# Gates by logarithm, exponential and a Newton step, and linear-attention steps at quarters of a chunk, in a two-layer hybrid encoder on one core

## The chip, the cores and the metric

The kernel runs on one core of one Trainium2 chip. The metric is the device time of one execution in microseconds (us). The engines are called by the profile's names: PE (TensorE matmuls), PEld (TensorE weight loads), ACT (ScalarE), DVE (VectorE), POOL (GpSimd) and SP (SyncE, which issues the DMAs here).

## The reference

Two encoder layers work on 272 tokens (256 and 16 learned meta tokens), model width 2048, all in float32. In each layer one projection makes the inputs of two groups of heads; their outputs are concatenated, projected, added to the residual and normalised; a squared-ReLU MLP of width 8192 and a second LayerNorm follow.

```python
def _layer(h, w_in, ...):
    proj = jnp.einsum('bld,dp->blp', h, w_in)
    gq, gk, gv, gr, glr, nq, nk, nv = jnp.split(proj, points, axis=-1)
    y_gla = _gla_mixer(gq, gk, gv, gr, glr, gla_w_up, gla_b_up, gla_norm_w)
    y_na = _na_mixer(nq, nk, nv, na_rel_bias)
    mix = jnp.einsum('blm,md->bld', jnp.concatenate([y_gla, y_na], axis=-1), w_out)
    h = _layer_norm(DEEPNORM_ALPHA * h + mix, ln1_w, ln1_b)
    ff = jnp.einsum('blf,fd->bld', jnp.square(jax.nn.relu(jnp.einsum('bld,df->blf', h, w_ff1))), w_ff2)
    return _layer_norm(DEEPNORM_ALPHA * h + ff, ln2_w, ln2_b)

# _gla_mixer, four heads, both directions: S_t = diag(a_t) S_{t-1} + k_t^T v_t,  o_t = q_t S_t
    o = (o_fwd + o_bwd)[:, pad:].reshape(B, L, GLA_HEADS, GLA_DV)
    o = o * lax.rsqrt(jnp.mean(jnp.square(o), axis=-1, keepdims=True) + LN_EPS) * norm_w
    o = o.reshape(B, L, GLA_HEADS * GLA_DV) * jax.nn.silu(r)
```

The neighbourhood attention (NA, 16 heads) lets each of the 4 x 64 grid tokens attend to a clamped window and to the meta tokens, with a relative bias. The meta tokens are dropped at the end, so layer 1 (the second) needs 256 columns of most results.

## The kernel before, in words

Activations lie as (128 features, tokens). A large product is made in three matmuls of rounded operands: high weight by high and by low activation, low weight by high activation (`three`, L151 to L162). With 272 columns these are L160, L161 and L162; with 256 columns high and low activations lie side by side and L156 takes both, L157 the third. A product of 128 output rows runs over 16 chunks of 128 input features, called chunks here.

**The weight stream.** Weights arrive as tiles of 128 x 1024 floats, eight chunks each. `made` (L137) issues a tile's DMA on SP, ACT casts its high part (`wh`, L147), DVE subtracts for the low part (`wl`, L148). `raw`, `wh` and `wl` have three buffers each, and `weights` keeps one tile ahead of the one in use.

**Background work.** `by_m` (L190) runs the products of one group of 512 output rows. After each eighth chunk and after each eviction it calls `pump(fg, bg)`, which adds to two credits and takes one step of the queue `fg` or `bg` per whole credit; a step is one stretch of a generator up to its `yield`. A step's instructions are placed in each engine's program behind the stream's so far, and DVE's behind the newest `wl` (`issue_after`). A builder with priorities settles the final order of each engine's instructions and the waits.

**The stage around the change.** After keys, values and queries, each layer runs two groups of 512 columns for the output gate r (`ev_r`), with `pump=(1, GLA_R)`, then six groups for NA (`ev_na`), with `pump=(1, GLA_NA)`. Beside them `bg` holds the whole linear attention (`gla`, L479), and `fg` the gates (`silu`, L417) and then the NA pairs (`na_pair`, L590). Before the sixth NA group whatever is left in `bg` is taken at once.

`gla` computes the scores of each of four heads by ten levels, distance classes in powers of two. A level is a chain over four engines: POOL makes differences of the running decay (`gaps`, L460; L447 to L450 at level 9), ACT takes their exponential (L471), DVE multiplies by q and k (L476), PE makes the scores (L505, and L507 for the meta rows; L498 and L500 at level 9), and DVE or ACT puts them into A by a mask (L519, L521). The chain runs ahead: two `gaps` and one `operands` are issued before their level's matmuls; the tile `lev` has three buffers. Scores with the 16 meta keys are collected in `Am`. At the end of a head `gla_out` (L529) zeroes a tile `am` on POOL (L533), stacks `Am` in it as high, low and high part (`stack`: ACT L214 twice, DVE L215), and in the next steps multiplies by the values (L542, L543 with A, L544 with `am`), takes the mean square (L776), and applies the norm, the gate and the rounding.

**The gate.** `ev_r` takes exp(-r) from PSUM on ACT (L411, tile `rs`), POOL adds one (L412), ACT copies r (L414, tile `rv`); `silu` inverts in two halves on DVE (L421) and multiplies by r (L424). There are eight gates a layer, 16 in all. `newton` (L427) is the LayerNorm's and `gla_out`'s inverse root: logarithm and exponential on ACT (L429, L430), and three DVE operations (L431 to L433). The one table set that ACT loads at the start holds both functions.

Of the kernel before, what the change touches and what calls it, by code (L numbers as in the profile page):

```python
# [2 lines left out]

# [11 lines left out]
P = 128  # L15
# [16 lines left out]
EPS = 1e-5  # L32
TAU = 16.0
NEG = -1e30
GLA_R, GLA_NA, NORMS = 1.3, 1.1, (1.0, 0.6)
LEAD = 4


# [9 lines left out]
class Trunk:  # L48
# [18 lines left out]
    def consts(self):  # L67
        nc, c = self.nc, self.cp
        t = lambda n, s, d=F32: c.tile(s, d, name=n, tag=n)
        self.vec = t("vec", [P, DEPTH, 66])  # L70
        nc.sync.dma_start(self.vec, self.i["vec"].rearrange("l p v -> p l v"))
        self.ident = t("ident", [P, P])
        nc.sync.dma_start(self.ident, self.i["ident"])
        self.sel = t("sel", [LRK, 2])
        nc.sync.dma_start(self.sel, self.i["sel"])
        self.qmask = t("qmask", [NM, NK2])
        nc.sync.dma_start(self.qmask, self.i["qmask"])
        self.mask = t("mask", [P, 7, P], U8)
        raw = self.wp.tile([P, WB], F32, name="raw", tag="raw")[:, :7 * P].rearrange("p (l c) -> p l c", l=7)
        nc.sync.dma_start(raw, self.i["mask"])  # L80
        nc.gpsimd.tensor_copy(self.mask, raw)
        self.ones = {}
        for n in (GDV, 4 * P, D):
            self.ones[n] = t(f"ones{n}", [P, P])
            nc.gpsimd.memset(self.ones[n], 1.0 / n)
        self.ones_r = {}
        for n in self.ones:
            self.ones_r[n] = t(f"onesr{n}", [P, P], F32R)
            nc.scalar.copy(self.ones_r[n], self.ones[n])
        self.eps = t("eps", [P, 1])  # L90
        nc.gpsimd.memset(self.eps, EPS)
        self.one = t("one", [P, 1])
        nc.gpsimd.memset(self.one, 1.0)

# [95 lines left out]
    def by_m(self, acts, ns, evict, pump=(0, 0), apart=False, renew=False):  # L190

        nk = len(acts)
        for m, n in enumerate(ns):
            ps = self.pm.tile([P, 512], F32, name="mm", tag="mm")
            for k in range(nk):
                if k % 8 == 0:
                    wh, wl = self.weights()
                self.three(ps, wh, wl, (k % 8) * P, acts[k], n, k == 0, k == nk - 1)
                if k % 8 == 7 and k < nk - 1:
                    self.pump(*pump)  # L200
                if renew and m == len(ns) - 1 and k == 8:
                    self.renew(2)
            parts = [ps[:, :T], ps[:, T:]] if n == T else [ps[:, :n]]
            evict(m, parts if apart else self.whole(parts))
            self.pump(*pump)

    def split(self, src, hi, lo):
        self.nc.scalar.copy(hi, src)
# [197 lines left out]
    def ev_r(self, c, ps):  # L406

        nc, n = self.nc, self.n
        self.y[c] = self.pair(self.yp, "y", c)
        s = self.g2.tile([P, L], F32, name="rs", tag="rs")[:, :n]  # L410
        nc.scalar.activation(s, ps, AF.Exp, scale=-1.0)  # L411
        nc.gpsimd.tensor_scalar(s, s, 1.0, 1.0, ALU.mult, ALU.add)  # L412
        r = self.g2.tile([P, L], F32, name="rv", tag="rv")[:, :n]
        nc.scalar.copy(r, ps)  # L414
        self.fg.append(self.silu(c, s, r))

    def silu(self, c, s, r):  # L417
        yield
        half = self.n // 2
        for p in (slice(0, half), slice(half, self.n)):  # L420
            self.nc.vector.reciprocal(s[:, p], s[:, p])  # L421
            yield
        gate = self.g2.tile([P, L], F32, name=f"gate{c}", tag=f"gate{c}", bufs=1)[:, :self.n]
        self.nc.vector.tensor_tensor(gate, r, s, ALU.mult)  # L424
        self.gate[c] = gate

    def newton(self, y, v, eps, t):  # L427
        nc = self.nc
# [50 lines left out]
    def gla(self):  # L479

        nc, n, full, g2 = self.nc, self.n, self.full, self.g2
        levels = (7, 0, 1, 2, 3, 4, 5, 6, 8, 9)
        todo = iter([(h, lv) for h in range(GH) for lv in levels])
        begun = [self.gaps(*next(todo)) for _ in range(2)]
        yield
        ahead = self.operands(*begun.pop(0))
        yield  # L490
        for h in range(GH):
            A = g2.tile([P, 6, P], F32, name="A", tag="A")
            Am = g2.tile([NM, L], F32, name="Am", tag="Am")
            for lv in levels:
                q, k = ahead
                ps = self.bank()
                if lv == 9:
                    nc.tensor.matmul(ps[:, :T], lhsT=k[:, T:T + P], rhs=q[:, :T], start=True, stop=True)  # L498
                    for b in range(2 * full):
                        nc.tensor.matmul(ps[:, T + b * NM:T + b * NM + NM], lhsT=k[:, b * P:b * P + P],  # L500
                                         rhs=q[:, T:L], start=True, stop=True)
                else:
                    for b in (slice(0, P), slice(P, T)):
                        r = b if lv < 8 else slice(P - b.start, T - b.start)
                        nc.tensor.matmul(ps[:, b], lhsT=k[:, b], rhs=q[:, r], start=True, stop=True)  # L505
                    if full and lv <= 4:
                        nc.tensor.matmul(ps[:, T:L], lhsT=k[:, T:T + P], rhs=q[:, T:L], start=True, stop=True)  # L507
                if begun:
                    ahead = self.operands(*begun.pop(0))
                nxt = next(todo, None)  # L510
                if nxt:
                    begun.append(self.gaps(*nxt))
                p2 = ps[:, :T].rearrange("p (s c) -> p s c", s=2)
                if lv == 9:
                    if full:
                        nc.vector.tensor_copy(A[:, 2:6:3, :NM], ps[:, T:T + 2 * NM].rearrange("p (s c) -> p s c", s=2))
                    nc.scalar.copy(Am[:, :T], ps[:NM, :T])
                elif lv >= 7:
                    nc.scalar.copy(A[:, 0:5:4, :] if lv == 7 else A[:, 1:4:2, :], p2)  # L519
                else:  # L520
                    nc.vector.copy_predicated(A[:, 0:5:4, :], self.mask[:, lv:lv + 1, :].to_broadcast([P, 2, P]), p2)  # L521
                if full and lv == 0:
                    nc.vector.tensor_copy(Am[:, T:L], ps[:NM, T:L])
                elif full and lv <= 4:
                    nc.vector.copy_predicated(Am[:, T:L], self.mask[:NM, lv, :NM], ps[:NM, T:L])
                yield
            yield from self.gla_out(h, A, Am)

    def gla_out(self, h, A, Am):  # L529

        nc, n, g2 = self.nc, self.n, self.g2
        am = g2.tile([80, L], F32R, name="am", tag="am")[:, :n]
        nc.gpsimd.memset(am.bitcast(F32), 0.0)  # L533
        self.stack(Am[:, :n], am, NM, (0, 64), 32)
        yield
        af = A.rearrange("p s c -> p (s c)")
        os_ = []
        sq = g2.tile([P, 2, L], F32, name="sq", tag="sq", bufs=1)
        for e in range(2):
            o = self.bank()[:, :n]  # L540
            c = slice(h * GDV + e * P, h * GDV + e * P + P)
            nc.tensor.matmul(o, lhsT=self.V[0][:, c], rhs=af[:, :n], start=True, stop=False)  # L542
            nc.tensor.matmul(o, lhsT=self.V[1][:, c], rhs=af[:, 384:384 + n], start=False, stop=False)  # L543
            nc.tensor.matmul(o, lhsT=self.VS[:, c], rhs=am, start=False, stop=True)  # L544
            nc.scalar.activation(sq[:, e, :n], o, AF.Square)
            os_.append(o)
            yield
        nc.vector.tensor_tensor(sq[:, 0, :n], sq[:, 0, :n], sq[:, 1, :n], ALU.add)
        ms = yield from self.mean(sq[:, 0, :n], GDV, pool=g2)
        rs = g2.tile([P, L], F32, name="grs", tag="grs", bufs=1)[:, :n]  # L550
        tn = g2.tile([P, L], F32, name="gtn", tag="gtn", bufs=1)[:, :n]
        self.newton(rs, ms, self.eps, tn)
        yield
        while 2 * h + 1 not in self.gate:
            yield
        for e in range(2):
            c = 2 * h + e
            hi, lo = (t[:, :n] for t in self.y[c])
            o = g2.tile([P, L], F32, name="on", tag="on")[:, :n]
            nc.vector.scalar_tensor_tensor(o, os_[e], self.vec[:, self.l, 64 + e:65 + e], rs, ALU.mult, ALU.mult)  # L560
            nc.vector.tensor_tensor(o, o, self.gate[c], ALU.mult)
            self.split(o, hi, lo)
            self.done.add(c)
            yield
# [458 lines left out]
```

## Time and profile before

| what | value |
|---|---|
| median of 3 runs | 2427.96 us (2427.77 to 2428.14) |
| the profiled execution | 2427.82 us, of which the span is 2425.8 us |
| granted clock, mean | 0.997 |
| layer 0: gate stage, NA and linear attention, to the output projection | about 110 to 380 us |
| layer 1: the same | about 1352 to 1600 us |
| HBM read | 412.57 MB, 171 GB/s with the writes over the span |

In a row of the profile's groups stand line, engine, operation, output and inputs, shapes and count, then busy us and mean ns of one, then the idle time of the engine just before them and what ended it. In a timeline row the start and duration in us come first, and a bracket gives the idle time before and what ended it. A list of waits gives who waited for whom, us in total, times and the longest. Idle time of an engine that is not the bottleneck costs nothing; the chain of work that ended last lies on PE for 94% of the span.

### The profile page before, as it was taken

What the parts mean: (1) busy time and instruction counts of PE and PEld (TensorE: products, weight loads), DVE (VectorE), ACT (ScalarE), POOL (GpSimd) and SP (SyncE); (2) the same over time, 40 slices, a digit from 0 to 9 for tenths busy, and PEclk for the clock granted to TensorE, in tenths of its full rate; (3) what the DMA queues carried; (4) which work ended last, traced back from release to release, by engine and by line L of the source; (5) the groups of instructions that cost most, each with busy time, mean ns of one, the idle gap of its engine ahead of it and who ended that gap; (6) DMA issues with size and microseconds to landing.
All of it is one profiled execution on the core that took longest, in us unless ns stands there. A gap on an engine that the chain in (4) does not pass through costs nothing.

```text
span 2425.8 us, 43082 instructions
## 1 busy us (share of the span) xinstructions
PE 2394.4 (99%) x17276; PEld 2270.6 (94%) x17276; DVE 1576.3 (65%) x2469; ACT 1189.2 (49%) x1962; POOL 285.7 (12%) x447
## 2 busy tenths in 40 slices
PE   9999999999999999999999999999999999999997
PEld 9999999999999999999999899999988888888886
DVE  6688777775544455546577787778866555666655
ACT  6555555564433344444456555555644333444443
POOL 1064420010000000000021444300200000000000
PEclk9999999999999999999999999999999999999998
DMA  7544444555555555555555444456566556556563
GB/s 243 165 133 155 145 133 158 172 179 175 174 175 174 175 177 174 177 175 173 176 168 186 144 156 150 136 156 191 184 190 184 190 189 187 189 185 189 186 189 129
DMA packets 118359, 417.46 MB, mean 172 GB/s; under 512 B 13388, under 2 KB 16332, under 8 KB 118160
## 3 DMA queue, kind: packets, MB, share of 16 engines
q1 hardware_dynamic: 118160, 414.72, 54.1%
q8 instruction: 135, 2.21, 0.4%
q14 instruction: 64, 0.52, 0.1%
HBM read 412.57 MB, written 2.10 MB: 171 GB/s over the span
## 4 chain that ended last, share of the span: by engine, by line
PE 94%; DVE 3%; issue 1%; ACT 1%; DMA 0%; POOL 0%; SPq 0%; ACTq 0%; DVEq 0%; POOLq 0%
PE mm L156 22%; PE mm L160 17%; PE mm L162 17%; PE mm L161 17%; PE mm L157 11%; PE mm L186 5%; PE bg L505 1%; DVE wl L148 1%; PE bg L652 1%; DVE acc L868 1%; PE bg L601 0%; POOL lev L460 0%; ACT wh L147 0%; PE bg L322 0%; PE bg L542 0%
## 5 line engine op out<-in xcount | busy, mean ns | idle before, releaser
L148 DVE TENSOR_TENSOR wl<-raw,wh 128x1024 fp32r<-128x1024 f32 (+1 forms) x772 | 946.0, 1226 | 654.6 <-ACT wh L147 646.2
L147 ACT CAST wh<-raw 128x1024 fp32r<-128x1024 f32 (+1 forms) x772 | 805.1, 1044 | 956.6 <-PE mm L161 405.6
L160 PE MATMUL mm<-x,wh 128*128 128x272 f32 (+2 forms) x2176 | 632.6, 291 | 0.0
L161 PE MATMUL mm<-x,wh 128*128 128x272 f32 (+2 forms) x2176 | 628.4, 289 | 0.0
L162 PE MATMUL mm<-x,wl 128*128 128x272 f32 (+2 forms) x2176 | 628.4, 289 | 0.0
L160 PEld LDWEIGHTS mm<-x,wh 128*128 128x128 f32 x2176 | 413.3, 190 | 1.4 <-issue 0.5
L162 PEld LDWEIGHTS mm<-x,wl 128*128 128x128 f32 x2176 | 410.6, 189 | 0.3
L161 PEld LDWEIGHTS mm<-x,wh 128*128 128x128 f32 x2176 | 410.0, 188 | 0.1
L156 PE MATMUL mm<-x,wh 128*128 128x512 f32 x1152 | 408.7, 397 | 0.0
L157 PE MATMUL mm<-x,wl 128*128 128x256 f32 x1152 | 324.5, 282 | 0.3 <-DVE wl L148 0.3
L156 PEld LDWEIGHTS mm<-x,wh 128*128 128x128 f32 x1152 | 217.7, 189 | 49.8 <-issue 0.6
L156 PE MATMUL mm<-y,wh 128*128 128x512 f32 x704 | 248.2, 393 | 0.1
L157 PEld LDWEIGHTS mm<-x,wl 128*128 128x128 f32 x1152 | 217.6, 189 | 0.8 <-DVE wl L148 0.8
L162 PE MATMUL mm<-y,wl 128*128 128x272 f32 x704 | 203.2, 289 | 0.0
L160 PE MATMUL mm<-y,wh 128*128 128x272 f32 x704 | 203.2, 289 | 0.0
L161 PE MATMUL mm<-y,wh 128*128 128x272 f32 x704 | 202.9, 288 | 0.0
L157 PE MATMUL mm<-y,wl 128*128 128x256 f32 x704 | 197.6, 281 | 0.5 <-DVE wl L148 0.5
L156 PE MATMUL mm<-u,wh 128*128 128x512 f32 x512 | 180.6, 393 | 0.0
L460 POOL TENSOR_TENSOR lev<-be 128x128 f32<-128x128 f32 (+1 forms) x256 | 151.9, 623 | 117.9 <-PE bg L505 49.8
L156 PEld LDWEIGHTS mm<-y,wh 128*128 128x128 f32 x704 | 131.8, 187 | 30.5 <-ACT wh L147 0.5
L162 PE MATMUL mm<-u,wl 128*128 128x272 f32 x512 | 147.8, 289 | 0.0
L160 PE MATMUL mm<-u,wh 128*128 128x272 f32 x512 | 147.8, 289 | 0.0
(234 smaller groups left out, 3327.9 us busy)
## 6 DMA issues: line engine op xcount, KB each, us to landing
raw<-in_wff SPq DMA_DIRECT2D x512, 512.0 KB, 3.6
raw<-in_win SPq DMA_DIRECT2D x190, 512.0 KB, 3.5
raw<-in_wout SPq DMA_DIRECT2D x64, 512.0 KB, 3.6
nb<-in_nab SPq DMA_DIRECT2D x16, 352.0 KB, 3.3
out<-acc SPq DMA_DIRECT2D x8, 256.0 KB, 2.2
xraw<-in_xT SPq DMA_DIRECT2D x7, 272.0 KB, 5.2
wraw<-in_wup SPq DMA_DIRECT2D x2, 392.0 KB
raw<-in_win SPq DMA_DIRECT2D x4, 128.0 KB, 2.8
```

What stands on the lines that cost most here:

```text
L147: nc.scalar.copy(wh[:, c], raw[:, c])
L148: self.wl = nc.vector.tensor_tensor(wl[:, c], raw[:, c], wh[:, c].bitcast(F32), ALU.subtract).ins
L156: mm(ps, lhsT=wh[:, c:c + P], rhs=x.both[:, :, :T], start=first, stop=False)
L157: mm(ps[:, T:], lhsT=wl[:, c:c + P], rhs=xh[:, :T], start=False, stop=last)
L160: mm(o, lhsT=wh[:, c:c + P], rhs=xh[:, :n], start=first, stop=False)
L161: mm(o, lhsT=wh[:, c:c + P], rhs=xl[:, :n], start=False, stop=False)
L162: mm(o, lhsT=wl[:, c:c + P], rhs=xh[:, :n], start=False, stop=last)
L186: self.nc.tensor.matmul(ps[m][:, :n], lhsT=parts[p][0][:, c:c + P], rhs=acts[j][parts[p][1]][:, :n], start=j + p == 0, stop=j == nk - 1 an ...
L460: tt = lambda o, x, y: nc.gpsimd.tensor_tensor(o, x, y, ALU.subtract)
L505: nc.tensor.matmul(ps[:, b], lhsT=k[:, b], rhs=q[:, r], start=True, stop=True)
L652: nc.tensor.matmul(r[hs], lhsT=(v2 if rest else v1)[:, t, hs], rhs=p2[:, t, :] if rest else p1[:, 2 * t + hh, :], start=rest, stop=not rest)
L868: return self.nc.vector.tensor_tensor(v, v, by[:, None, :].to_broadcast([P, m, n]), alu)
```

## The change

There are three parts.

1. *Gates.* POOL now clamps exp(-r) at 1e38 and adds one, ACT's copy of r is negated, and instead of two reciprocals DVE's work is a Newton step: ACT makes y = exp(-ln d) with the scale 2^-64 and its counterpart in the bias (a new constant `down`), DVE then forms d*y, (d*y - 2)*y and the product with -r. `silu` has two stops where it had three.
2. *Steps.* In `by_m` the background credit is added at four points of a product, after chunks 4, 8 and 12 and after the eviction, half as much each; foreground steps stay at two points. `GLA_NA` rises from 1.1 to 1.25.
3. *Meta scores.* `am` is zeroed and stacked in the step of level 9, where `Am` is completed, and no longer in the step behind it; `gla_out` keeps an empty step in that place.

```diff
-GLA_R, GLA_NA, NORMS = 1.3, 1.1, (1.0, 0.6)
+GLA_R, GLA_NA, NORMS = 1.3, 1.25, (1.0, 0.6)
+BIG = 1e38
...
+        self.down = t("down", [P, 1])
+        nc.gpsimd.memset(self.down, -64 * math.log(2))
...
-                if k % 8 == 7 and k < nk - 1:
-                    self.pump(*pump)
+                if k % 8 == 3:
+                    self.pump(0, pump[1] / 2)
+                elif k % 8 == 7 and k < nk - 1:
+                    self.pump(pump[0], pump[1] / 2)
...
-            self.pump(*pump)
+            self.pump(pump[0], pump[1] / 2)
...
-        s = self.g2.tile([P, L], F32, name="rs", tag="rs")[:, :n]
-        nc.scalar.activation(s, ps, AF.Exp, scale=-1.0)
-        nc.gpsimd.tensor_scalar(s, s, 1.0, 1.0, ALU.mult, ALU.add)
+        d = self.g2.tile([P, L], F32, name="rd", tag="rd")[:, :n]
+        nc.scalar.activation(d, ps, AF.Exp, scale=-1.0)
+        nc.gpsimd.tensor_scalar(d, d, BIG, 1.0, ALU.min, ALU.add)
         r = self.g2.tile([P, L], F32, name="rv", tag="rv")[:, :n]
-        nc.scalar.copy(r, ps)
-        self.fg.append(self.silu(c, s, r))
+        nc.scalar.activation(r, ps, AF.Copy, scale=-1.0)
+        self.fg.append(self.silu(c, d, r))
 
-    def silu(self, c, s, r):
-        yield
-        half = self.n // 2
-        for p in (slice(0, half), slice(half, self.n)):
-            self.nc.vector.reciprocal(s[:, p], s[:, p])
-            yield
-        gate = self.g2.tile([P, L], F32, name=f"gate{c}", tag=f"gate{c}", bufs=1)[:, :self.n]
-        self.nc.vector.tensor_tensor(gate, r, s, ALU.mult)
-        self.gate[c] = gate
+    def silu(self, c, d, r):
+        yield
+        nc = self.nc
+        y = self.g2.tile([P, L], F32, name=f"gate{c}", tag=f"gate{c}", bufs=1)[:, :self.n]
+        nc.scalar.activation(y, d, AF.Ln, scale=2.0 ** -64)
+        nc.scalar.activation(y, y, AF.Exp, scale=-1.0, bias=self.down)
+        yield
+        nc.vector.tensor_tensor(d, d, y, ALU.mult)
+        nc.vector.scalar_tensor_tensor(d, d, -2.0, y, ALU.add, ALU.mult)
+        nc.vector.tensor_tensor(y, d, r, ALU.mult)
+        self.gate[c] = y
...
                     nc.scalar.copy(Am[:, :T], ps[:NM, :T])
+                    am = g2.tile([80, L], F32R, name="am", tag="am")[:, :n]
+                    nc.gpsimd.memset(am.bitcast(F32), 0.0)
+                    self.stack(Am[:, :n], am, NM, (0, 64), 32)
...
-            yield from self.gla_out(h, A, Am)
+            yield from self.gla_out(h, A, am)
 
-    def gla_out(self, h, A, Am):
+    def gla_out(self, h, A, am):
         nc, n, g2 = self.nc, self.n, self.g2
-        am = g2.tile([80, L], F32R, name="am", tag="am")[:, :n]
-        nc.gpsimd.memset(am.bitcast(F32), 0.0)
-        self.stack(Am[:, :n], am, NM, (0, 64), 32)
         yield
```

More of the change, by code (lines that the diff above doesn't have):

```diff
@@ L1 @@
+import math
 from collections import deque
```

## The prediction

> **What bounds the kernel now.** I read the page first, then the busy time of chosen stretches, then what TensorE (PE) waited for, then its timeline at those waits.
>
> ```profile
> span 2425.8 us, 43082 instructions
> ...
> PE 2394.4 (99%) x17276; PEld 2270.6 (94%) x17276; DVE 1576.3 (65%) x2469; ACT 1189.2 (49%) x1962; POOL 285.7 (12%) x447
> ...
> L148 DVE TENSOR_TENSOR wl<-raw,wh 128x1024 fp32r<-128x1024 f32 (+1 forms) x772 | 946.0, 1226 | 654.6 <-ACT wh L147 646.2
> L147 ACT CAST wh<-raw 128x1024 fp32r<-128x1024 f32 (+1 forms) x772 | 805.1, 1044 | 956.6 <-PE mm L161 405.6
> ```
>
> PE is busy for nearly the whole span, and the change adds and removes no matmul, so the most it can gain is PE's waiting. The last two rows are the weight stream: each tile costs ACT 1.04 us and DVE 1.23 us. The busy table (PE, PEld, DVE, ACT, POOL, granted clock, DMA share, GB/s) shows where the stream is at its best and where not:
>
> ```profile
> 600.00:700.00 100.00, 100.00 (x798) 100.00 (x797) 50.54 (x59) 41.46 (x55) 0.00 (x0) 1.00 0.55 174
> 1900.00:2000.00 100.00, 100.00 (x574) 87.63 (x573) 51.14 (x54) 37.53 (x36) 0.00 (x0) 1.00 0.60 188
> 1352.00:1420.00 68.00, 64.15 (x401) 57.00 (x400) 58.40 (x85) 38.68 (x71) 39.87 (x68) 1.00 0.46 146
> ```
>
> In the MLP a tile of eight chunks takes 24 x 100/798 = 3.0 us in layer 0 (three matmuls a chunk) and 16 x 100/574 = 2.8 us in layer 1 (two). The third row is layer 1's output-gate stage, with the linear attention (GLA) beside it: DVE is busy 86% of it and PE loses time. The five longest of what PE waited for in layer 1 from there to the output projection (us, times, longest; two more of 0.3 and 0.2 follow them):
>
> ```profile
> PE bg L544 <- ACT rs L411: 1.7, 1, 1.7
> PE bg L505 <- DVE lev L476: 1.2, 2, 1.0
> PE bg L652 <- DVE p L642: 0.8, 1, 0.8
> PE bg L776 <- ACT sp L208: 0.8, 1, 0.8
> PE bg L498 <- ACT rv L414: 0.6, 1, 0.6
> ```
>
> L544 multiplies the stacked meta scores (am), L505 and L498 are levels of the score matrix. These figures leave out the modelled tail of the matmul before, so I size the large ones from start to start on PE's timeline:
>
> ```profile
> 152.08 0.62 PE L543 MATMUL bg<-A,V 128*128 128x272 f32 x2
> 153.77 0.36 PE L544 MATMUL bg<-am,VS 80*128 80x272 f32 x1 [1.06 <-DVE am L215]
> ...
> 157.45 0.62 PE L543 MATMUL bg<-A,V 128*128 128x272 f32 x2
> 157.71 0.49 PE L544 MATMUL bg<-am,VS 80*128 80x272 f32 x1
> ...
> 1368.27 0.60 PE L505 MATMUL bg<-lev 128*128 128x128 f32 x4
> 1369.89 0.57 PE L505 MATMUL bg<-lev 128*128 128x128 f32 x3 [1.02 <-DVE lev L476]
> ...
> 1384.83 0.59 PE L543 MATMUL bg<-A,V 128*128 128x256 f32 x2
> 1387.13 0.35 PE L544 MATMUL bg<-am,VS 80*128 80x256 f32 x1 [1.71 <-ACT rs L411]
> ...
> 1409.88 0.71 PE L505 MATMUL bg<-lev 128*128 128x128 f32 x4 [0.18 <-DVE lev L476]
> 1410.35 0.37 PE L160 MATMUL mm<-x,wh 128*128 128x272 f32 x1
> ```
>
> Undisturbed, L543's start to L544's is 157.71 - 157.45 = 0.26 us, and a level of four passes takes 1410.35 - 1409.88 = 0.47. So am cost 1.69 - 0.26 = 1.43 us in layer 0 and 2.30 - 0.26 = 2.04 in layer 1, and the late level 1.62 - 0.47 = 1.15. The other late level cost 0.2 (its bracket). All that the change can reach: 1.43 + 2.04 + 1.15 + 0.2 + 0.8 + 0.8 + 0.6 = 7.0 us, plus perhaps 2 us of shorter waits that the brackets cut off: a ceiling near 9.
>
> **The change, part by part.** *Meta scores.* Both am waits come from the attention's step that stacks am and the step that uses it falling in one pump, with only L542 and L543 between. The stacking now stands in the step before. In the changed program's order 36 stream matmuls (4.5 us) lie between layer 0's first L498 and L542, and 24 (4.2 us) in layer 1. In the six heads where the steps were a tile apart already there is no such wait in the list. Gain 1.43 + 2.04 = 3.5; bounds 2 to 3.5. The same ACT, DVE and POOL instructions are issued, only sooner.
>
> *Quarter steps.* The program's order shows levels singly, 24 and 12 matmuls apart in layer 0 (16 and 8 in layer 1), where two used to follow each other. A level that came too soon gets 1.4 us more, above the 1.15 that was missing. Gain 1.15 + 0.2 = 1.35. L776 now stands alone behind a whole tile: 0.8. L652 and L498 were late because ACT and DVE stood in queues behind GpSimd (POOL); spacing helps, but nothing excludes the same again, so half of 1.4: 0.7. The finer mixing makes 193 stream runs out of 171; a return from a level to the stream shows no extra time above (0.47 for four passes), so 0, at most 22 x 0.1 = 2. The faster step rate in neighbourhood attention empties the GLA queue before its last group of columns; none of the waits listed stands there, so 0.
>
> *Gates.* Rows of the tile that is inverted (min/median/max ns), with LayerNorm's logarithm and exponential of that name:
>
> ```profile
> L421 DVE RECIPROCAL rs<-rs x32: 894/953/1002, 121.2 to 1433.7; 128x136 f32<-128x136 f32 x16, 128x128 f32<-128x128 f32 x16
> ...
> L412 POOL TENSOR_SCALAR rs<-rs x16: 404/494/1397, 120.0 to 1419.0; 128x272 f32<-128x272 f32 x8, 128x256 f32<-128x256 f32 x8
> L424 DVE TENSOR_TENSOR gate<-rv,rs x16: 415/434/675, 126.8 to 1434.7; 128x272 f32<-128x272 f32 x8, 128x256 f32<-128x256 f32 x8
> ...
> L429 ACT ACTIVATE rs<-var,eps x4: 508/516/524, 475.7 to 2409.9; 128x272 f32<-128x272 f32 x2, 128x256 f32<-128x256 f32 x2
> L430 ACT ACTIVATE rs<-rs x4: 417/425/433, 476.2 to 2410.5; 128x272 f32<-128x272 f32 x2, 128x256 f32<-128x256 f32 x2
> ```
>
> DVE loses 32 x 0.95 = 30.5 us and gains two more operations a gate, 32 x 0.43 = 13.9: net -16.6, some -8 of them in the third stretch above, which leaves DVE 50 of 68 us. ACT gains 16 x (0.52 + 0.43) = 15.1, there 7.6, to 46 of 68. POOL's operation changes its arithmetic, not its count. Both engines stay under PE's 64, so the busy time costs nothing; it pays only through the waits counted above.
>
> What it adds is a wait. ACT takes its instructions in the order written, and the logarithm, behind the gate's copy, needs POOL's L412; behind it queue the next wh cast, level exponentials and evictions, for which DVE's wl and then PE wait. Whether POOL was free when L412 was wanted, in layer 1 (1352:1420), then in layer 0 (110:210):
>
> ```profile
> POOL rs L412 <- ACT rs L411: 44.3, 7, 35.5
> ```
>
> ```profile
> POOL rs L412 <- ACT rs L411: 20.0, 2, 10.6
> ```
>
> POOL idled until ACT's exponential in 7 of 8 gates in layer 1 and 2 of 8 in layer 0. With POOL free the logarithm waits 0.49 us, most of it under the copy. With POOL behind a level it waits up to
>
> ```profile
> 1355.72 1.47 POOL L460 TENSOR_TENSOR lev<-be 128x128 f32<-128x128 f32 x4
> ...
> 1381.90 2.90 POOL L460 TENSOR_TENSOR lev<-be 128x128 f32<-128x128 f32 x4
> ```
>
> 2.90 + 0.49, and with logarithm and exponential ACT is held 4.3 us. The cover is the three-deep weight stream: two tiles are in hand (5.6 us in layer 1, 6.0 in layer 0) when the next cast may start, and cast and subtraction need 2.27, so 3.3 to 3.7 us are to spare. A worst catch costs 0.6 to 1.0 us, a usual one nothing. I charge two such catches of 0.65, 1.3 us; ends 0 and 16 x 0.8 = 12.8, and I stand near 0 because seven of layer 1's eight found POOL free and layer 0 hardly waits now.
>
> [...] L460's four subtractions took 1.47 us at best and 2.90 at worst: they are slowed by something beside them. [...] My sum leaves the blocking at 0, since spaced levels have 1.4 us more to come in, and gives 2421.8; with the blocking in full it gives 2428.7, as the second rival works out from rows.
>
> **Sum.** The gains are 3.5 + 1.35 + 0.8 + 0.7 = 6.35, and 1.0 more for half of the 2 us of shorter waits, which spacing and a lighter DVE should also reach: 7.35. Less 1.3 for the logarithm's wait that is -6.05. The profiled execution took 2427.82 us (span 2425.8 and 2.0 around it), 0.14 under the median of the runs, 2427.96, so 2427.82 - 6.05 = 2421.8 us.
>
> **Rivals.** *Only am goes* (0.15): the loop from PE's release of a level's buffer over POOL, ACT and DVE back to PE is the limit, and the other waits come back elsewhere. For it: POOL's levels slow to 2.90; against: only two of all levels were late by more than 0.1 us. Time 2427.82 - 3.5 = 2424.3.
>
> *POOL is blocked by the gates* (0.12): two more two-input DVE operations of 0.43, 0.86 us a gate, delay a level in each of layer 1's eight gates: 6.9 us back, 2421.8 + 6.9 = 2428.7, no change. For it: L460's spread; against: DVE hands back 1.9 us of reciprocal a gate, and 1.4 us of spacing covers 0.86. [...]
>
> *ACT becomes the wait* (0.18), slower: in the gate stages the logarithms catch POOL in a batch every time, 16 x 0.8 = 12.8 us, less the 7.35 of gains: +5.45, 2433.3. From 7.35/16 = 0.46 us lost a gate the kernel is slower than before. For it: layer 0, where six gates in eight found POOL occupied; against: layer 1's seven in eight.
>
> That the change does not do what it says is excluded by the changed program's order, in which every part is seen.
>
> **Numbers.** The forecast has 0.55: 2421.8, its own range 2418.8 (the ceiling of 9) to 2423.1 (no shorter waits gained). A difference under 0.2%, 4.9 us, I call no change: the forecast counts as faster, the first two rivals as the same (0.27), the last as slower (0.18). The range 2418.3 to 2430 leaves out the dearer part of the last rival and little else.
>
> **What would show it.** Right: no wait of L544 for am; L505 and L776 gone from PE's list; DVE near 1560 and ACT near 1204 us busy; layer 1's gate stage shorter by some 5 us. Wrong: ACT idle behind POOL's min-and-add ahead of the logarithm with wh late and PE waiting at L156 or L157 for wl; L460 over 0.62 us on average; or waits of the old size on other levels.

## The result, and the profile after

The changed kernel takes 2459.16 us (median of 4 runs, 2457.83 to 2460.64), the kernel before 2428.05 beside it on the same chip (2427.77 to 2428.51): ratio 1.0128 (95% interval 1.0111 to 1.0146), 31 us slower. Its profiled execution took 2460.12 us. From its page:

```profile
span 2458.2 us, 43091 instructions
...
PE 2407.5 (98%) x17276; PEld 2280.5 (93%) x17276; DVE 1563.7 (64%) x2469; ACT 1203.0 (49%) x1994; POOL 293.2 (12%) x448
```

The same 17276 matmuls, DVE lighter by 12.6 us, ACT heavier by 13.8, and a span 32.4 us longer. The busy table says where: layer 1's gate stage, and the MLP for comparison.

```profile
1363.80:1438.40 74.60, 67.66 (x401) 59.33 (x401) 57.52 (x92) 44.93 (x87) 50.85 (x69) 0.95 0.42 133
...
600.00:700.00 100.00, 100.00 (x797) 100.00 (x796) 51.65 (x61) 42.72 (x60) 0.00 (x0) 1.00 0.56 174
```

The MLP is unchanged (797 matmuls, 798 before). The changed kernel reaches layer 1's gate stage 11.7 us late, so the first row starts that much later than before's 1352.00; its 401 matmuls take 74.6 us where they took 68.0, at a granted clock of 0.95 instead of 1.00. What PE waited for, longest first (us, times, longest):

```profile
PE bg L514 <- DVE lev L485: 5.6, 4, 2.7
PE bg L514 <- DVE nv L638: 5.6, 3, 3.3
PE bg L553 <- DVE am L221: 5.4, 3, 3.3
...
PE bg L661 <- DVE p L651: 3.7, 2, 2.5
PE bg L553 <- ACT wh L151: 2.8, 1, 2.8
```

Lines have moved by a few: L514 is before's L505 (a level's matmul), L553 is L544 (am), L661 is L652, L221 is L215; the start of the kernel (4.8 us, 4.5 before) is left out. The largest wait in the stages around the change was 1.7 us before; now there are several of 2.5 to 3.3. Counted from one matmul's start to the next, gaps of over 0.6 us are 21 with together 35.1 us; before they were 11 with 13.2. These figures hold the matmul that begins each gap too; the page gives the exact account. PE's idle time grew from 31.4 to 50.7 us, by 19.3, and its busy time by 13.1 for the same matmuls; together that is the 32.4.

The 13.1 is nearly all the clock. Before, the trace has the granted clock at 1.00 from 8.9 us to the last matmul. Here it falls to 0.50 five times, for 3.4 or 6.8 us, 23.9 us together: by estimate half of that, about 12 us, of work lost. The first, in three windows of the busy table (the clock is the number behind POOL's pair):

```profile
208.60:212.00 3.40, 0.30 (x2) 0.33 (x3) 2.97 (x9) 3.35 (x8) 0.00 (x0) 1.00 0.03 10
212.00:215.40 3.40, 3.40 (x18) 3.40 (x17) 1.79 (x4) 1.93 (x4) 0.00 (x0) 0.50 0.78 176
215.40:218.80 3.40, 3.40 (x26) 3.24 (x24) 2.66 (x6) 1.63 (x5) 0.32 (x1) 1.00 0.57 182
```

PE stands still for 3.1 us and then works one stretch at half clock: 18 matmuls against 26 in the next.

Two chains from the timeline show how such a wait comes about. The one just seen:

```profile
199.32 0.66 ACT L480 ACTIVATE lev<-lev 128x544 f32<-128x544 f32 x1 [4.26 <-POOL lev L459]
...
200.02 0.94 DVE L485 TENSOR_TENSOR lev<-lev,qk 128x544 f32<-128x544 f32 x1 [3.52 <-ACT lev L480]
...
206.19 0.44 ACT L593 ACTIVATE ns<-ns,nst 128x176 f32<-128x176 f32 x1 [2.83 <-DVE nst L591]
...
207.74 0.62 PE L552 MATMUL bg<-A,V 128*128 128x272 f32 x2
...
208.54 0.34 ACT L526 COPY Am<-bg 16x256 f32<-16x256 f32 x1
208.79 1.04 ACT L151 CAST wh<-raw 128x1024 fp32r<-128x1024 f32 x1
...
209.74 0.85 ACT L220 CAST am<-Am 16x272 fp32r<-16x272 f32 x2
209.86 1.23 DVE L152 TENSOR_TENSOR wl<-raw,wh 128x1024 fp32r<-128x1024 f32 x1 [0.32 <-ACT wh L151]
...
211.12 0.43 DVE L221 TENSOR_TENSOR am<-Am,am 16x272 fp32r<-16x272 f32 x1
...
211.70 0.36 PE L553 MATMUL bg<-am,VS 80*128 80x272 f32 x1 [3.34 <-DVE am L221]
```

It begins with level 9, POOL's longest (L456 to L459, before's L447 to L450): its exponential waits 4.26 us for POOL, and DVE stands 3.52 us behind it. In the order of time, DVE then comes late to NA's scores. ACT stands 2.83 us for their row maxima (`nst`) and does the softmax's exponentials; only behind them come the copy of `Am`, a weight cast and am's casts, and on DVE am's subtraction stands behind `wl`. PE had asked for am 3.3 us earlier. The second, in layer 1:

```profile
1556.16 2.30 POOL L456 TENSOR_SCALAR lev<-be 128x256 f32<-128x256 f32 x1
...
1559.08 1.14 POOL L459 TENSOR_SCALAR lev<-be 128x256 f32<-128x256 f32 x1
1560.26 0.66 ACT L480 ACTIVATE lev<-lev 128x544 f32<-128x544 f32 x1 [3.41 <-POOL lev L459]
...
1562.02 0.38 ACT L635 COPY v<-bg 128x256 f32<-128x256 f32 x1
...
1563.35 0.92 DVE L638 COPY nv<-bg 48x64 f32<-48x64 f32 x4
...
1564.42 0.98 PE L514 MATMUL bg<-lev 128*128 128x128 f32 x3 [3.33 <-DVE nv L638]
```

Here level 9's exponential holds the head of ACT's queue for 3.41 us; behind it wait a weight cast and NA's copy out of PSUM, behind these DVE's copies (`nv`), and PE's next level waits for them. Level 9's hold itself is not new: its eight exponentials waited 28.8 us for POOL in the kernel before and wait 29.7 here. So the cost lies in what now stands behind them.

### The profile page after: what moved, and what is told of

It is laid out like the page before. It is cut to its first block, busy times and chain, and to the rows that moved or that the text cites. A ratio compares the mean times of both kernels' runs of the same rounds, so it can differ in the third digit from the quotient of the medians.

```text
span 2458.2 us, 43091 instructions
## 1 busy us (share of the span) xinstructions
PE 2407.5 (98%) x17276; PEld 2280.5 (93%) x17276; DVE 1563.7 (64%) x2469; ACT 1203.0 (49%) x1994; POOL 293.2 (12%) x448
## 4 chain that ended last, share of the span: by engine, by line
PE 87%; issue 4%; DVE 4%; POOL 4%; ACT 1%; DMA 0%; SPq 0%; ACTq 0%; POOLq 0%; DVEq 0%
PE mm L160 21%; PE mm L164 16%; PE mm L165 15%; PE mm L166 15%; PE mm L161 11%; PE mm L190 6%; POOL lev L469 2%; DVE wl L152 1%; PE bg L514 1%; PE bg L661 1%; DVE acc L877 1%; ACT wh L151 1%; POOL rd L418 0%; PE bg L610 0%; PE bg L328 0%
```

## The experiments

Every time below stands beside runs of the kernel before on the same chip (medians 2427.67 to 2428.05); differences are given against these, and between two changed kernels as the difference of their medians. My theory at the start was that the logarithm behind POOL costs most, the rivals that the steps or am do. The first four runs take the change apart.

**Gates alone.** The first part of the diff and nothing else.

```diff
...
-        nc.gpsimd.tensor_scalar(s, s, 1.0, 1.0, ALU.mult, ALU.add)
+        nc.gpsimd.tensor_scalar(d, d, BIG, 1.0, ALU.min, ALU.add)
...
-        self.fg.append(self.silu(c, s, r))
+        self.fg.append(self.silu(c, d, r))
...
```

> Part 1 alone: the gates by logarithm, exponential and Newton step, all else as before. Theory G (the gates: ACT's logarithm waits for POOL with the weight casts behind it, and silu's two stops in place of three bring the neighbourhood-attention pairs forward among the attention's levels): 2440 to 2450 us, with half-clock stretches in the record. Theory S (the steps): 2424 to 2429, no half-clock stretch before the end. Theory M (the meta stack): as S.

Measured: 2439.55 us, ratio 1.0048 (1.0033 to 1.0063): 11.8 us slower.

**Steps alone.**

```diff
-GLA_R, GLA_NA, NORMS = 1.3, 1.1, (1.0, 0.6)
+GLA_R, GLA_NA, NORMS = 1.3, 1.25, (1.0, 0.6)
...
+                if k % 8 == 3:
+                    self.pump(0, pump[1] / 2)
...
```

> Part 2 alone: background credit at quarters and the rate 1.25. Theory S (levels come sooner than POOL, ACT and DVE can feed them while the pairs of neighbourhood attention stand in the same queues): 2445 to 2458 us. Theory G: 2424 to 2430. Theory M: 2424 to 2430.

Measured: 2444.04 us, ratio 1.0067 (1.0050 to 1.0084): 16.3 us slower, with three half-clock stretches of 3.4 us.

**Meta scores alone.**

```diff
                     nc.scalar.copy(Am[:, :T], ps[:NM, :T])
+                    am = g2.tile([80, L], F32R, name="am", tag="am")[:, :n]
+                    nc.gpsimd.memset(am.bitcast(F32), 0.0)
+                    self.stack(Am[:, :n], am, NM, (0, 64), 32)
...
```

> Part 3 alone: the meta scores stacked in the step of level 9. Theory M (the stack's two casts and a subtraction now stand among the softmax's work and come late): 2433 to 2442 us. Theories S and G: 2424 to 2427, the 3.5 us of the two waits of L544 saved and no other.

Measured: 2427.84 us, ratio 1.0000 (0.9991 to 1.0009): nothing. Its timeline at layer 1's am:

```profile
1384.37 0.63 ACT L471 ACTIVATE lev<-lev 128x512 f32<-128x512 f32 x1 [1.76 <-POOL lev L460]
1384.54 1.21 DVE L148 TENSOR_TENSOR wl<-raw,wh 128x1024 fp32r<-128x1024 f32 x1
1384.90 0.82 ACT L214 CAST am<-Am 16x256 fp32r<-16x256 f32 x2
...
1386.11 0.42 DVE L215 TENSOR_TENSOR am<-Am,am 16x256 fp32r<-16x256 f32 x1
```

The stack, though written a step earlier, still stands behind a level's exponential that waits for POOL, and behind `wl` on DVE. Both waits for am are as long as before (1.49 and 2.10 us from start to start).

**Steps and meta scores, no gates.** The diff without its first part.

> Parts 2 and 3 without part 1. Theory G: 2422 to 2430 us, the loss gone. Theory S: 2445 to 2458. Theory M: 2433 to 2445.

Measured: 2442.80 us, ratio 1.0062 (1.0047 to 1.0077): 15.0 us slower. So the gates cost 12 us alone and 16 on top of the rest, the steps 15 to 16 without the gates and 19 on top of them, am nothing. Neither the gates nor the steps are the whole cause, as each theory had it; alone they add to 28 of the 31.

Next, each half of the steps.

```diff
-GLA_R, GLA_NA, NORMS = 1.3, 1.1, (1.0, 0.6)
+GLA_R, GLA_NA, NORMS = 1.3, 1.25, (1.0, 0.6)
```

> Halves of a chunk as before, NA's rate 1.25 in place of 1.1: the second half of the steps alone. Steps in quarters and rate together cost 16.3 us. Theory: the rate is the smaller part, because it moves only the attention stage and its two half-clock stretches in that stage cost some 3 to 4 us: 2430 to 2435. Rival, the rate is the whole cost, because heads' steps close up until a head's exponential is due before POOL's products are done: 2442 to 2445. The prediction's own price for it was nothing: 2428.

Measured: 2432.70 us, ratio 1.0020 (1.0011 to 1.0029): 4.8 us slower.

```diff
-                if k % 8 == 7 and k < nk - 1:
-                    self.pump(*pump)
+                if k % 8 == 3:
+                    self.pump(0, pump[1] / 2)
+                elif k % 8 == 7 and k < nk - 1:
+                    self.pump(pump[0], pump[1] / 2)
...
-            self.pump(*pump)
+            self.pump(pump[0], pump[1] / 2)
```

> Quarters of a chunk alone, rates as before (1.3 and 1.1). Theory: quarters are the larger part, because a step now stands right before or in the middle of a chunk's matmuls, where the level's exponentials have had a quarter of a chunk less to come: 2436 to 2442. Rival, quarters cost nothing by themselves and only the rate does: 2427 to 2429. The prediction's price was a gain of 4 us: 2424.

Measured: 2429.59 us, ratio 1.0008 (0.9999 to 1.0017). The theory expected 8 to 14 us and got 1.7; neither half explains the 16.3. Quarters alone remove the late levels of L505, as intended, but PE's largest wait in the stages is then another, 3.2 us in four times for NA's transposed scores `p`, and one of 1.1 us for level 9 is new. The cost of the steps is in the meeting of the two.

The gates have two possible causes: the missing stop in `silu`, which brings the NA pairs forward, or POOL's addition ahead of the logarithm. The next two edits are shown against the gates alone.

```diff
         nc.scalar.activation(y, y, AF.Exp, scale=-1.0, bias=self.down)
         yield
+        yield
         nc.vector.tensor_tensor(d, d, y, ALU.mult)
```

> The gates without reciprocal alone, with one more stop in them, so that each gate takes as many steps of the foreground as before and attention's pairs start where they did. Gates alone cost 11.8 us. Theory: the cost is what stands in ScalarE's queue (the logarithm behind GpSimd's addition), so the stop changes little: 2436 to 2441. Rival, the cost comes from attention's pairs being brought forward by the missing stops: 2427 to 2431.

Measured: 2437.35 us, ratio 1.0040 (1.0027 to 1.0052): the stop gives back 2.2 of the 11.8.

```diff
-        nc.gpsimd.tensor_scalar(d, d, BIG, 1.0, ALU.min, ALU.add)
...
-        nc.scalar.activation(y, d, AF.Ln, scale=2.0 ** -64)
-        nc.scalar.activation(y, y, AF.Exp, scale=-1.0, bias=self.down)
+        nc.scalar.activation(y, d, AF.Ln, bias=self.one)
+        nc.scalar.activation(y, y, AF.Exp, scale=-1.0)
...
-        nc.vector.tensor_tensor(d, d, y, ALU.mult)
+        nc.vector.scalar_tensor_tensor(d, d, 1.0, y, ALU.add, ALU.mult)
```

> The gates without reciprocal alone, and the addition of one taken from GpSimd: the logarithm adds it as its bias, the Newton step's first operation on VectorE adds it again; the limit at 1e38 is left out (no value of this data reaches it). As many operations on ScalarE and VectorE as in gates alone, none on GpSimd, and no wait of the logarithm for GpSimd (13 waits of together 15.9 us in the changed kernel). Theory: the logarithm's wait in ScalarE's queue is the cost of the gates (11.8 us), so most of it goes: 2427 to 2432. Rival, attention's pairs brought forward, or the two added passes on ScalarE, cost it: 2437 to 2441.

Measured: 2426.74 us, ratio 0.9997 (0.9988 to 1.0006): 12.8 us less than the gates with POOL, for one POOL instruction a gate (the limit at 1e38 is left out with it). PE's waits but for the start of the kernel, first in gates alone and then here (L512 and L511 are before's L505, L659 and L658 its L652, L551 and L550 its L544):

```profile
PE bg L512 <- DVE lev L483: 7.1, 6, 1.8
...
PE bg L659 <- DVE p L649: 2.8, 2, 1.4
PE bg L551 <- ACT rd L415: 2.4, 1, 2.4
```

```profile
PE bg L550 <- ACT rd L415: 2.9, 1, 2.9
PE bg L658 <- DVE p L648: 1.7, 2, 0.8
PE bg L511 <- DVE lev L482: 1.6, 1, 1.6
```

The levels are nearly in time again (7.1 to 1.6 us); a wait of 2.9 us for am stays. POOL's instruction ahead of the logarithm was the cost of the gates. How it costs is seen in two forms in the trace of gates alone:

```profile
1378.59 1.07 POOL L416 TENSOR_SCALAR rd<-rd 128x256 f32<-128x256 f32 x1 [4.02 <-ACT rd L415]
...
1382.22 0.63 ACT L478 ACTIVATE lev<-lev 128x512 f32<-128x512 f32 x1 [2.11 <-POOL lev L467]
...
1419.26 0.42 ACT L426 ACTIVATE gate<-rd 128x256 f32<-128x256 f32 x1 [2.77 <-POOL rd L416]
1419.59 0.61 ACT L478 ACTIVATE lev<-lev 128x512 f32<-128x512 f32 x1
```

At 1419 the logarithm holds ACT for 2.77 us with a level's exponential right behind it, and PE waits for that level. At 1378 POOL is the one that is held: it stands for exp(-r) and then works 1.07 us while the next level's differences (L467) stand behind in its order, and the exponential is late without the logarithm. POOL's instruction took 23.2 us in all there, 11.8 in the kernel before. The edit takes both away, so the run does not say how much each cost. For the first as the larger: the logarithm waits 16.4 us for POOL in gates alone, while the exponentials' waits for POOL's differences are no longer than before (100.4 us together, 107.3 before).

For the steps, the chain of level 9 shown above was the suspect; the trace of the steps alone has it at the same place.

```diff
         if lv == 9:
             bm, e0 = bf[:, L - 1:L], eb[:, 0:1]
-            ts = nc.gpsimd.tensor_scalar
+            ts = nc.vector.tensor_scalar
```

> The steps alone (quarters and rate 1.25 together, 16.3 us slower), with level 9's four differences on VectorE instead of GpSimd. In the trace of the steps alone the long waits of TensorE (3.0 us for nv, 1.7 for nv, 1.9 for lev) each stand behind level 9's exponential, which holds the head of ScalarE's queue for 3.2 to 4.4 us until GpSimd has written level 9's differences; three half-clock stretches of 3.4 us come right after such waits. Theory: it is this head of the queue that costs the steps, so with the differences there early most of the 16.3 us goes: 2427 to 2433. Rival: the quarters bring heads' and pairs' steps together whatever the level, and the waits stay: 2439 to 2445.

Measured: 2429.70 us, ratio 1.0007 (0.9998 to 1.0016): 14.3 of the 16.3 us gone. PE's waits but for the start of the kernel, in the steps alone and with the edit (L507, L654 and L500 are before's L505, L652 and L498):

```profile
PE bg L507 <- DVE nv L631: 4.7, 2, 3.0
PE bg L654 <- DVE p L644: 3.7, 4, 2.3
PE bg L500 <- DVE lev L476: 3.0, 2, 1.9
```

```profile
PE bg L654 <- DVE p L644: 3.6, 4, 2.3
PE mm L157 <- DVE wl L148: 2.8, 3, 1.8
```

The waits for `nv` and level 9's `lev` are gone; the one for `p` stays. Level 9's exponential, which is the cause in question, waits half as long as in the steps alone:

```profile
ACT lev L473 <- POOL lev L452: 30.2, 8, 5.1
```

```profile
ACT lev L473 <- DVE lev L452: 14.9, 8, 4.2
```

Not all of the 14.3 us need be level 9's. One of the three half-clock stretches in the trace of the steps alone follows the wait for `p`; that wait is as long with the edit (2.60 and 2.61 us from start to start) and draws none there. The control, the same edit on the kernel before:

> The kernel before, with level 9's differences on VectorE and nothing else: the control for the steps. Theory: in the kernel before, level 9's exponential waits 28.8 us on 8 times too, but little of TensorE's time hangs on it (1.2 us of waits for lev), so 2426 to 2428.5. Rival: the edit gains over 8 us by itself, and then it says nothing of the steps: below 2420.

Measured: 2425.39 us, ratio 0.9990 (0.9981 to 0.9999): 2.3 us by itself, a little more than expected, so some 12 of the 14.3 belong to the steps.

Does this carry the whole change? On the changed kernel, first the gates without POOL, then level 9 on DVE as well:

> The whole change, with the gates' addition of one taken from GpSimd (the logarithm adds it as its bias, VectorE adds it again; the limit at 1e38 is left out, which no value here reaches). Done to the gates alone this took 12.8 us off. Theory: the parts add, so 2459 less 12 to 13: 2444 to 2449. Rival: in the whole change the same waits hang on other queue heads as well (level 9, attention's softmax), and less than half comes back: 2453 to 2458.

Measured: 2443.31 us, ratio 1.0063 (1.0051 to 1.0076): 15.9 us less than the changed kernel.

> The whole change, with both causes taken away: the gates' addition of one on ScalarE and VectorE instead of GpSimd (the limit at 1e38 left out), and level 9's differences on VectorE. Theory: the first leaves 2443.3, the second takes 14.3 us off the steps: 2427 to 2432. Rival: together the parts make waits that neither has alone: 2436 to 2443.

Measured: 2428.07 us, ratio 1.0003 (0.9994 to 1.0012): all 31 us are gone, and no half-clock stretch is left. The two causes, both of them POOL's work that ACT waits for, carry the whole loss of the change. Its parts are not free even so: on the kernel before, the two edits gained 1.2 and 2.3 us, and here nothing is left of that.

The waits for am can be had in another way.

```diff
-            nc.tensor.matmul(o, lhsT=self.VS[:, c], rhs=am, start=False, stop=True)
-            nc.scalar.activation(sq[:, e, :n], o, AF.Square)
             os_.append(o)
+            if e:
+                for i, u in enumerate(os_):
+                    c = slice(h * GDV + i * P, h * GDV + i * P + P)
+                    nc.tensor.matmul(u, lhsT=self.VS[:, c], rhs=am, start=False, stop=True)
+                    nc.scalar.activation(sq[:, i, :n], u, AF.Square)
             yield
```

> The kernel before, with the matmul on the meta scores' stack (am) one step later: both halves' products with V first, then both products with am. As many instructions and steps; the stack has a whole step more to come. Theory: the waits for am, 1.4 us in layer 0 and 2.1 us in layer 1 from one matmul's start to the next, and the smaller ones go: 2424 to 2425.5. Rival: the squares, which now come one after the other, are late for the mean in their place: 2427 to 2429.

Measured: 2424.71 us, ratio 0.9987 (0.9978 to 0.9996): 3.3 us, the size the prediction gave these waits. Put on the changed kernel beside the other two edits:

> As the kernel before this one in the list, and the matmul on the stack am one step later (3.3 us off the kernel before by itself). Theory: 3 to 5 us less than the kernel with both causes taken away: 2423 to 2428. Rival: the whole change holds no waits for am that were not already gone: the same time.

Measured: 2426.69 us, ratio 0.9996 (0.9987 to 1.0005): 1.4 us less than without it, not the 3 to 5 expected; there is no wait for am among the longest there, so the rival was nearer. And the best of it together, without the steps and the earlier stacking:

> The gates without reciprocal and without GpSimd, the matmul on the stack am one step later, and level 9's differences on VectorE; steps in halves and rates as in the kernel before. Theory: beside the gates' 2426.7 the wait of 3.25 us for am with the half-clock stretch of 3.4 us behind it goes (together 4.9 us), and 1 us of waits for lev: 2420 to 2423, below both kernels. Rival: as with each reordering so far, new waits take their place: 2426 to 2430.

Measured: 2422.26 us, ratio 0.9976 (0.9966 to 0.9985): 5.7 us below the kernel before, the fastest of all. The changed kernel with all three edits, which differs from it by the steps and the earlier stacking alone, lies 1.0 us below its kernel before: those two still cost 4.8 us together.

```profile
PE 2392.4 (99%) x17276; PEld 2271.2 (94%) x17276; DVE 1569.0 (65%) x2501; ACT 1200.2 (50%) x1994; POOL 248.3 (10%) x400
```

Against the changed kernel DVE and ACT are as busy as they were; only POOL has less (293 to 248 us). Over the whole span it was 12% busy; in layer 1's gate stage, where it counts, it was 50.9 of 74.6 us in the changed kernel (table above).

Last, the half clock by itself: waits put into the MLP, where there are none.

```diff
                 self.three(ps, wh, wl, (k % 8) * P, acts[k], n, k == 0, k == nk - 1)
+                if slow and (m, k) == (1, 2):
+                    w, r = slow
+                    for _ in range(r):
+                        self.nc.gpsimd.tensor_copy(wh[:, 2 * P:2 * P + w], wh[:, 2 * P:2 * P + w].bitcast(F32))
```

> The kernel before, with 16 waits put into the second half of the feed-forward (eight in each layer, about 22 us apart): GpSimd copies a piece of a weight chunk onto itself between two matmuls that read it, pieces of 128 to 768 columns, so that TensorE stands still for some 1 to 3.5 us. It measures the half clock by itself. Theory: it follows the length of the standstill wherever it is: none behind waits up to 2.0 us, a stretch of 3.4 us at half clock behind those over 2.6, so the span grows by the waits and by 1.7 us for each stretch, some 50 us together. Rival: it belongs to the attention stages and their load: no stretch in any of the 16 places.

Measured: 2449.1 us (one run). Twelve of the places show as standstills of 1.29 to 1.95 us from one matmul's start to the next, and no stretch at half clock follows any of them. In the second run a place holds one standstill of 1.8 to 2.5 us, or two of 0.7 to 1.9 us with a few matmuls between:

> As the run with 16 put-in waits (which were 1.3 to 2.1 us from one matmul's start to the next and drew no half clock), with two to four of GpSimd's copies in place of one, so that the waits are some 2.2 to 4.5 us or more. Theory: half clock follows the length of the standstill wherever it is: none below 2.1 us, a stretch of 3.4 us or 6.8 us behind every wait of 3.4 us or more, some of those between. Rival: it needs the attention stages, and there is no stretch in the feed-forward however long the wait.

Measured: 2474.85 us (one run), and four stretches of 3.4 us at half clock in the MLP. So it isn't the attention stage, but it isn't the length of one wait either: the longest single one, 2.52 us, drew none, and two of 1.03 and 1.31 shortly behind each other did. Waits over 3.4 us did not come about. The clock's record was then read in all the traces: all changes of the clock within a trace lie whole multiples of 3.4133 us apart (in the changed kernel's eleven, the first at 212.02 and the last at 2444.33 us, 654 multiples between them). The busy table cut at that grid, first from the run with short waits, then from the one with long ones:

```profile
2229.80:2233.20 3.40, 1.95 (x9) 1.21 (x8) 2.15 (x3) 1.42 (x3) 1.89 (x1) 1.00 0.73 173
2233.20:2236.60 3.40, 3.40 (x21) 2.97 (x20) 1.41 (x2) 1.05 (x2) 0.00 (x0) 1.00 0.33 135
```

```profile
2203.70:2207.10 3.40, 1.76 (x7) 1.04 (x7) 2.89 (x4) 0.56 (x2) 3.27 (x3) 1.00 0.39 148
2207.10:2210.50 3.40, 3.30 (x10) 2.83 (x11) 0.32 (x1) 0.00 (x0) 0.04 (x1) 0.50 0.36 145
```

What went with a half-clock window was how much of the grid window before it PE stood still, as summed from the gaps of over 0.6 us between matmul starts, each less 0.25 us for the matmul that begins it. The 2.52 us lay across two windows. In 19 traces 18 windows at full clock had 2.0 us or more of it, and behind 17 of them came a window at half clock; of 16 with 1.65 to 1.92 us four had one; behind windows with less, none. In the two windows shown the sums are 1.70 and 2.06 us.

## Why the prediction was wrong, point by point

- *Meta scores, -3.5: wrong in the edit, right in the size.* Alone they gave 0. The program's order did put the stacking 24 and 36 matmuls earlier in PE's count, but the step of reasoning "only sooner" ignored that on ACT and DVE it stays behind what holds the head of the queue: in the run of am alone a level's exponential, 1.76 us behind POOL, and a `wl` of 1.21 us. Moving the consumer instead gave 3.3. In the changed kernel the wait for am that should have vanished is one of the longest, 3.3 us.
- *Quarter steps, -2.85: not gained.* Quarters alone cost 1.7 us (from -0.2 to 4.1); the late levels went and the waits came back on `p`. That is the mechanism of the rival in which only am goes, with am failing too. The 1.0 us for shorter waits was not gained either: the changed kernel has 21 gaps of over 0.6 us, the kernel before 11.
- *The faster rate, 0: wrong.* Alone it cost 4.8 us, with the quarters the two cost 16.3. That it empties the GLA queue earlier was right; that nothing stands in its way was not. It sets level 9 beside NA's pairs, and both share ACT's queue; this was tried on the two steps together, and for the rate alone it is inferred.
- *The logarithm, 1.3: the hold was foreseen, its size and its path were wrong.* 11.8 was measured for the gates alone, and 12.8 came back when POOL's instruction was left out. That this is the upper end, 16 x 0.8 = 12.8, is luck, since the 0.8 was priced by the weight casts. Two steps failed. I took seven of eight gates with POOL idle as proof that POOL would be in time, "the logarithm waits 0.49 us, most of it under the copy". POOL was idle, in 13 of 16 gates, and yet the logarithm waited in 13, 15.9 us in all, some 1.2 us each, because POOL's operation itself is longer (before 0.40, 0.49, 1.40 us at least, median and most; here 1.07, 1.42, 2.11):

```profile
POOL rd L418 <- ACT rd L417: 80.3, 13, 47.9
...
ACT gate L428 <- POOL rd L418: 15.9, 13, 1.7
```

```profile
L418 POOL TENSOR_SCALAR rd<-rd x16: 1065/1424/2112, 120.0 to 1425.8; 128x272 f32<-128x272 f32 x8, 128x256 f32<-128x256 f32 x8
```

And I measured the hold against the cover of the weight stream, two tiles in hand. That cover held: in these stages PE waits for `wl` 0.5 us in one place. The loss falls on the background's matmuls (levels, `nv`, `p`, am), which have no such cover. Whether min and add, or the engines beside it, make POOL's operation longer was not tried. (The hold behind a level was also read too short: 2.90 us is not the worst of L460's four subtractions in the kernel before; those at 297.16 took 3.61.)
- *ACT becomes the wait, the slower rival at 0.18:* its direction and its engine came true, by more than its 2433.3, because the gates were only one of two such holds and because of the clock; the path did not, as the point above says.
- *POOL blocked by DVE, the rival at 0.12:* not seen in the levels. Their subtractions take as long as before, 630 ns on average against 623 (L460); the limit of 0.62 that I set was passed by the kernel before already:

```profile
L469 POOL TENSOR_TENSOR lev<-be 128x128 f32<-128x128 f32 (+1 forms) x256 | 153.2, 630 | 125.8 <-PE bg L514 65.9 <-DVE be L353 47.3 <-PE bg L516 4.0
```

In both traces such a subtraction took 0.39 to 0.48 us where no TENSOR_TENSOR or SCALAR_TENSOR_TENSOR of DVE ran beside it (93 of the 256 before, 71 here), and where one did 0.39 to 3.15 us before, 0.75 on average, and 0.39 to 2.55 here, 0.71 on average. So the slow ones stand beside DVE's two-input work, but did so before the change too. The 6.9 us that this rival charged for the gates' share are shown by no run; what the runs showed in their place is the mean longer by 7 ns. Whether that work lengthened L418 stays open.
- *Busy times:* DVE near 1560 and ACT near 1204 came as said (1563.7 and 1203.0), and so did what they are worth: with POOL's part taken away, the gates' lighter DVE gains 1.2 us (2.9 gained to 1.5 lost), which is not clear of noise.
- *The ceiling of 9 us held:* the best kernel gains 5.7. What was missing is a floor. Nothing in the sum bounded what a wait could cost, and five of the six gaps of over 2 us brought a half-clock stretch of 3.4 or 6.8 us, by estimate half of it in work. (The upper end of my own range, 2423.1, was added wrongly as well: without the shorter waits the sum gives 2422.8.)

## What to carry to other kernels

A wait at the head of an engine's queue was charged here to what stood queued behind it: the logarithm's 2.77 us behind POOL to a level's exponential and to PE, level 9's 3.41 us to a weight cast, a copy out of PSUM and PE. Before putting an instruction that depends on a slow engine (here POOL, 12% busy over the whole span) on a shared queue (here ACT), list what stands behind it and how far ahead each of those consumers runs; the best-covered stream says nothing about the others (PE waited 0.5 us for `wl` in these stages, and up to 3.3 us for the background's operands). Writing work earlier in the program did not move it past the head of such a queue (0 us gained); moving its consumer later gave it the time (3.3 us). Where edits to pacing brought two chains onto one queue, the costs of the parts did not add from their single runs (4.8 and 1.7 us alone, 16.3 together): find the instruction that holds the head and move that (14.3 us came back).

## What the runs showed of the hardware

The half clock was not in my sum. Behind a window of 3.4133 us in which PE stood still for 2.0 us or more came a window at half clock in 17 of 18 cases, in one gap or in two, by estimate 1.7 us of work lost (half of 3.4); behind 1.64 us or less came none in all 19 traces. In the changed kernel's own trace the five sums are 3.10, 2.00, 2.24, 2.35 and 2.63 us, each with half clock behind it, and the largest without it 1.66. The kernel before was close to these sums without showing it: in the window with its am wait, below, PE stood still 1.84 us, and the next kept the full clock.

```profile
1384.40:1387.80 3.40, 1.69 (x10) 1.22 (x9) 3.34 (x6) 2.55 (x6) 0.80 (x2) 1.00 0.61 200
1387.80:1391.20 3.40, 3.40 (x21) 2.97 (x20) 2.68 (x4) 1.69 (x4) 0.00 (x0) 1.00 0.59 193
```
